# Group B's norm on single columns of tokens, the rotation's transfers on GpSimd's queue, the sums of x on VectorE, and more side steps ahead of transposes, in one step of a hybrid encoder layer

## The chip, the cores and the metric

One core of a Trainium2 chip. The time is device microseconds of a whole execution; of several executions the median is given. The engines of the core are TensorE (PE; its weight loads are PEld), VectorE (DVE), ScalarE (ACT), GpSimd (POOL) and SyncE (SP), which here only issues transfers. Every engine works through its own instructions in order and waits for others by semaphores.

## The reference

One layer for 512 prompt tokens and 8 streams of 16 new tokens, 640 tokens in all, in f32, model width 2048:

```python
xn = rmsnorm(x, norm_mix)
qa, ka, va, qb, kb, vb = split_proj(xn @ w_in)        # widths 1024 x 4, 128, 128
qb, kb = rope_partial(qb, pos), rope_partial(kb, pos) # first 16 of 64 dims of a head
oa = band_attend(qa, ka, va, bias=rel_bias)           # A: 16 heads, own chunk of 64 and 8 before
ob = band_attend(qb, kb, vb, sink=sinks)              # B: 16 q heads on 2 kv heads, window 128
o = concat(rmsnorm(oa, norm_grp_a), rmsnorm(ob, norm_grp_b))
x = x + o @ w_out
h = rmsnorm(x, norm_ffn)
x = x + (silu(h @ w_gate) * (h @ w_up)) @ w_down
return rmsnorm(x, norm_final), ...                    # and the new keys and values
```

The 16 new tokens of a stream attend to a cache of 256 (A) or 128 (B) earlier tokens and to each other; `rmsnorm` is x * rsqrt(mean(x*x) + 1e-6) * g.

## The kernel before

Activations lie transposed: 128 features on the partitions, 640 tokens as two halves of 320 in the columns. Each f32 product of a weight block and an activation tile is three matmuls (`mm3`, L246 to L248): high by high, high by low, low by high, where the high half of the weights is a copy on ScalarE (L237) and the low half a subtraction on VectorE (L238), both 128x1024. `dense` (L258) loads weights, splits them and runs such triples for one block of outputs; its results lie in PSUM tiles named dn, of which there are two, until VectorE multiplies them out. All other PSUM results lie in one of four banks named at.

Most projections into group A, and the feed-forward, go by `quartet`, a scheme of seven products of half size for a product of 2 by 2 blocks, of which the inputs need sums and differences. Those of x are made by `combine` (L943), for eight pairs of tiles: two subtractions on GpSimd (L957, L959), two steps on VectorE (L956, L963), and splits.

The main stream is a sequence of `dense` and `quartet` calls. Side work is written as Python generators, in streams named heads (attention of prompt tokens, `prompt_b` and `prompt_a`), decode (attention of new tokens, `decode_b` and `decode_a`), combine and norm. After each inner step of `dense` a counter rises by `n.rate` (0.55 to 2.5 by stage) and for each whole unit one generator is run to its next `yield`. So a yield more puts more matmuls of the main stream between two pieces of side work, and delays all that the stream does later. A `yield "part"` marks a piece that may be run beside another stream's. Then a scheduler orders each engine's instructions, within rules that keep TensorE's side work at the place where it was written.

In order of time: group B's keys, values and queries are projected, with `rope` (L611) on keys and on the eight query tiles. `rope` fills a tile with zeros on GpSimd, makes four transfers of 8x640 into it through SP's queue (L615, L616), and does three steps on VectorE (L617 to L619). `project_b` stores the new tokens' part of each query tile to memory (`sb_d`, L931), where `decode_b` reads it (L645 on) and GpSimd turns it (L646). `prompt_b` makes scores (L463), their maximum (L466), exponentials on ScalarE (L479), a scaling on VectorE (L484), transposes on TensorE (L376, in `flip`), a copy on ScalarE (L493), and weighs the values (L503). `decode_b` does the same for four steps of two streams each (scores L655, exponentials L668, scaling L673, transposes L376, copies L698, weights by values L707), and stores its output (L718). Then come the quartets, and at the last of them group A's attention starts.

Group B's norm (`norm_b`, L1041) adds the squares of the eight tiles of B's outputs on VectorE (`add`, L883), and runs `wide_steps` (L305), which leaves rsqrt of the mean, 128x640 with equal rows, in `r_b`: one matmul against ones for each half (L311), an affine step (L312), a square root on ScalarE (L314), a reciprocal and a correction in three steps on VectorE (L317 to L320), all on 128x320. The output blocks m = 0, 1, 2, ... of `w_out_b` run meanwhile; the results of m=0 and m=1 wait in the two dn tiles for `r_b` (L1098, then the addition of x, L1099), and m=1's are taken out only after the norm has been written out to its end. Group A's attention and decode run beside it: its copies of turned keys and values are at L629, its exponentials at L479 too, decode A's softmax at L757 to L764 (L761 to L768 after the change, as all lines behind the first edit move by 3, and by 4 to 6 further on).

`rstd_steps` (L276), which group A's norm and the last norm use, gives the same by single columns: matmuls with the tokens as weights and a column of ones as data (L284) give 128 tokens on the partitions and one column for each of six blocks of tokens; the arithmetic on VectorE and ScalarE is on 128x6 (L286 to L291); six matmuls against an identity (L297) spread it back to 128x640, and ScalarE copies it (L303).

## Time and profile before

| | |
|---|---|
| median of 3 runs | 2505.01 us (2503.35 to 2506.9) |
| profiled execution: time, span | 2504.86 us, 2503.1 us |
| granted TensorE clock | 0.998 |
| busy: TensorE, its weight loads | 99%, 96% |
| busy: VectorE, ScalarE, GpSimd | 79%, 42%, 23% |
| mean of memory traffic | 159 GB/s |

The rows of the trace are read so: start in us, length in us, engine, line of the kernel, operation, output and input by their names in the program, shapes, and in brackets the time that the engine stood idle just before and what ended it. The wait tables give, for an instruction and what it waited for, the sum of the idle time, the number of waits and the longest. A matmul with f32 operands leaves two records. Pieces of the chain that ended last have a start, a length and a place.

### The profile page before, as it was taken

The page shows a single profiled execution, that of the slowest core. Times are in us where ns is not written, and L with a number is a line of the kernel's source. Part 1 is how long each engine was busy: PE and PEld are TensorE (multiplying, and loading weights), DVE is VectorE, ACT ScalarE, POOL GpSimd, SP SyncE. Part 2 cuts the span into 40 slices and gives each one's busy share as a digit, 9 for nine tenths or more (in the row PEclk, how much of TensorE's full clock was granted, in tenths as well). Part 3 has the DMA queues.
Part 4 walks back from the last instruction along what each step waited for, and adds up shares of the span by engine and source line. Part 5 has one row for each costly group of instructions (what it writes and reads, how often), then busy time and mean ns, then how long its engine had stood idle before and what let it go on. Part 6 is the DMA issues. An engine that isn't in the chain of part 4 may idle for free.

```text
span 2503.1 us, 44475 instructions
## 1 busy us (share of the span) xinstructions
PE 2470.1 (99%) x17279; PEld 2410.7 (96%) x17279; DVE 1972.3 (79%) x3014; ACT 1056.3 (42%) x1701; POOL 575.7 (23%) x504
## 2 busy tenths in 40 slices
PE   9999999999999999999999999999999999999997
PEld 8888999987899999999999999999999999999997
DVE  7667777785658887788888888888888877777898
ACT  5445333365545543443344343434334333333343
POOL 1001000001002033333333232323232233333212
PEclk9999999999999999999999999999999999999999
DMA  5233533478664334543344344334437765665656
GB/s 200 89 93 119 173 135 125 144 254 288 218 213 158 133 117 147 173 141 121 125 147 133 128 133 143 124 130 132 147 122 237 245 194 167 175 170 167 199 165 195
DMA packets 191123, 401.67 MB, mean 160 GB/s; under 512 B 22496, under 2 KB 83296, under 8 KB 190912
## 3 DMA queue, kind: packets, MB, share of 16 engines
q1 hardware_dynamic: 163888, 339.69, 41.5%
q0 software_dynamic: 23424, 53.59, 7.8%
q10 hardware_dynamic: 3600, 5.55, 0.6%
q8 instruction: 136, 2.23, 0.4%
q14 instruction: 75, 0.61, 0.1%
HBM read 311.14 MB, written 86.87 MB: 159 GB/s over the span
## 4 chain that ended last, share of the span: by engine, by line
PE 91%; DVE 4%; DMA 2%; ACT 1%; issue 1%; POOL 0%; SPq 0%; DVEq 0%; ACTq 0%; POOLq 0%
PE dn L246 18%; PE dn L248 18%; PE dn L247 18%; PE at L246 10%; PE at L248 10%; PE at L247 10%; PE at L376 2%; PE at L503 1%; PE at L463 1%; DVE W L238 1%; DMA W<-w_down 1%; PE at L799 0%; DMA S<-x_d 0%; DVE S L466 0%; ACT W L237 0%
## 5 line engine op out<-in xcount | busy, mean ns | idle before, releaser
L237 ACT ACTIVATE W<-W 128x1024 fp32r<-128x1024 f32 (+2 forms) x662 | 640.5, 968 | 1059.8 <-PE dn L247 570.6
L246 PE MATMUL dn<-S,W 128*128 128x320 f32 x3374 | 1054.2, 313 | 2.0 <-ACT W L237 1.9
L248 PE MATMUL dn<-S,W 128*128 128x320 f32 x3374 | 1043.5, 309 | 1.9 <-DVE W L238 1.9
L247 PE MATMUL dn<-S,W 128*128 128x320 f32 x3374 | 1043.5, 309 | 0.3 <-DVE S L238 0.3
L238 DVE TENSOR_TENSOR W<-W,W 128x1024 fp32r<-128x1024 f32 (+2 forms) x662 | 772.4, 1167 | 95.4 <-ACT W L237 87.7
L246 PEld LDWEIGHTS dn<-S,W 128*128 128x128 f32 x3374 | 633.9, 188 | 17.5 <-issue 13.7
L248 PEld LDWEIGHTS dn<-S,W 128*128 128x128 f32 x3374 | 633.3, 188 | 3.8 <-DVE W L238 2.9
L247 PEld LDWEIGHTS dn<-S,W 128*128 128x128 f32 x3374 | 633.8, 188 | 1.7 <-issue 0.9
L246 PE MATMUL at<-S,W 128*128 128x320 f32 x1834 | 567.1, 309 | 0.7 <-ACT W L237 0.6
L248 PE MATMUL at<-S,W 128*128 128x320 f32 x1834 | 566.9, 309 | 0.6 <-DVE W L238 0.6
L247 PE MATMUL at<-S,W 128*128 128x320 f32 x1834 | 566.7, 309 | 0.0
L246 PEld LDWEIGHTS at<-S,W 128*128 128x128 f32 x1834 | 344.3, 188 | 1.3 <-ACT W L237 1.3
L248 PEld LDWEIGHTS at<-S,W 128*128 128x128 f32 x1834 | 344.3, 188 | 1.2 <-DVE W L238 1.2
L247 PEld LDWEIGHTS at<-S,W 128*128 128x128 f32 x1834 | 344.3, 188 | 0.0
L864 POOL TENSOR_TENSOR W<-W,W 128x1024 f32<-128x1024 f32 (+2 forms) x63 | 138.6, 2200 | 561.0 <-DVE W L238 360.9
L883 DVE TENSOR_TENSOR S<-S,dn 128x320 f32<-128x320 f32 x398 | 182.4, 481 | 73.3 <-PE dn L248 70.8
L883 DVE TENSOR_TENSOR S<-S,at 128x320 f32<-128x320 f32 x292 | 138.4, 483 | 81.8 <-PE at L248 79.2
L873 POOL TENSOR_TENSOR W<-W,W 128x1024 f32<-128x1024 f32 (+2 forms) x63 | 141.9, 2253 | 94.2 <-DVE W L238 93.0
L1176 POOL DMA_DIRECT2D S<-act_d x161 | 86.7, 539 | 282.0 <-PE dn L248 122.6
L857 DVE TENSOR_TENSOR W<-W,W 128x1024 f32<-128x1024 f32 (+2 forms) x86 | 117.2, 1362 | 37.9 <-DMA W<-w_gate 29.0
L861 DVE TENSOR_TENSOR W<-W,W 128x1024 f32<-128x1024 f32 (+2 forms) x86 | 94.6, 1100 | 57.0 <-DMA W<-w_up 30.5
L1240 DVE TENSOR_TENSOR S<-S,half 128x320 fp32r<-128x320 f32 x147 | 119.9, 836 | 2.3 <-ACT half L1238 0.4
(178 smaller groups left out, 1687.4 us busy)
## 6 DMA issues: line engine op xcount, KB each, us to landing
S<-act_d POOLq DMA_DIRECT2D x161, 320.0 KB, 3.7
W<-w_gate SPq DMA_DIRECT2D x88, 512.0 KB
W<-w_up SPq DMA_DIRECT2D x88, 512.0 KB
W<-w_in SPq DMA_DIRECT2D x66, 512.0 KB
W<-w_down SPq DMA_DIRECT2D x64, 384.0 KB
act_d<-half SPq DMA_DIRECT2D x147, 160.0 KB
act_d<-S SPq DMA_DIRECT2D x147, 160.0 KB
W<-w_down SPq DMA_DIRECT2D x68, 320.0 KB
```

The costliest lines, as they stand in the source:

```text
L237: self.nc.scalar.activation(hi, src, AF.Identity)
L238: self.nc.vector.tensor_tensor(lo, src, f(hi), ALU.subtract)
L246: mm(out, a[0], b[0], start=first, stop=False)
L247: mm(out, a[0], b[1], start=False, stop=False)
L248: mm(out, a[1], b[0], start=False, stop=last)
L857: nc.vector.tensor_tensor(b12[:, w], b12[:, w], b22[:, w], sub)
L861: nc.vector.tensor_tensor(s6[:, w], b11[:, w], b12[:, w], sub)
L864: eng.tensor_tensor(b11[:, w], b22[:, w], s6[:, w], sub)
L873: eng.tensor_tensor(b21[:, w], b21[:, w], s6[:, w], sub)
L883: add = lambda o, a, b: nc.vector.tensor_tensor(o, a, b, ALU.add)
L1176: nc.gpsimd.dma_start(out=r(sh(t, 2, HT)), in_=r(act_d[which, :, j]))
L1240: nc.vector.tensor_tensor(r(src), src, hi, ALU.subtract)
```

## The change

Six edits. `prompt_b` gets its mark "part" ahead of the first group of scores, and for the last query tile ahead of both, and one yield more behind the scores of the first and the last tile. `rope` issues its four transfers on GpSimd's queue, and `project_b` its store. `decode_b` gets one more yield ahead of the first turn, and five in place of four ahead of the transposes of each step. `combine` does its two subtractions on VectorE. `norm_b` yields four times in place of once, and uses `rstd_steps`, with six yields behind each of its steps.

```diff
--- before.py
+++ after.py
@@ -557,9 +557,12 @@
         for rr in range(2):
             t0, t1 = n.get("S"), n.get("S")
             heads.append(((t0, t1), [t0[:, 512:640], t0[:, :256], t0[:, 256:512], t1[:, :256]], n.small(4)))
-        yield "part"
         for blocks in ([(0, 0, 128), (1, 0, 256)], [(2, 128, 384), (3, 256, 512)]):
+            if blocks[0][0] == 0 or t == 7:
+                yield "part"
             scores(q, kb, blocks, [mask_b] * 2, heads)
+        if t in (0, 7):
+            yield
         yield
         for rr, (_, es, mx) in enumerate(heads):
             softmax(es, mx, sinks[:, 8 * rr + t:8 * rr + t + 1])
@@ -612,8 +615,8 @@
         rot = n.get("S")
         nc.gpsimd.memset(rot[:80], 0.0)
         for b in (0, 64):
-            dma(out=rot[b:b + 8], in_=x[b + 8:b + 16])
-            dma(out=rot[b + 8:b + 16], in_=x[b:b + 8])
+            nc.gpsimd.dma_start(out=rot[b:b + 8], in_=x[b + 8:b + 16])
+            nc.gpsimd.dma_start(out=rot[b + 8:b + 16], in_=x[b:b + 8])
         nc.vector.tensor_tensor(x[:80], x[:80], cos[:80], ALU.mult)
         nc.vector.tensor_tensor(rot[:80], rot[:80], sin[:80], ALU.mult)
         nc.vector.tensor_tensor(x[:80], x[:80], rot[:80], ALU.add)
@@ -677,13 +680,14 @@
 
         parts = [load(0)]
         yield
+        yield
         turn(parts[0][0], parts[0][3])
         yield "part"
         weights = score(0)
         for step in range(4):
             if step == 0:
                 parts.append(load(1))
-            for _ in range(4):
+            for _ in range(5):
                 yield
             if step == 0:
                 turn(parts[1][0], parts[1][3])
@@ -928,7 +932,7 @@
     def project_b(t):
         q = proj(26 + t, "Q", qps.pop(0) if qps else None, 0.125)
         rope(q)
-        dma(out=sb_d[:, t], in_=q[:, SP:])
+        nc.gpsimd.dma_start(out=sb_d[:, t], in_=q[:, SP:])
         heads_of(prompt_b, t, [("Q", q)], q)
 
     def keep_a(i, p, x):
@@ -942,7 +946,7 @@
 
     def combine(k0, k1):
 
-        tt, st = nc.gpsimd.tensor_tensor, nc.vector.scalar_tensor_tensor
+        tt, st = nc.vector.tensor_tensor, nc.vector.scalar_tensor_tensor
         third = n.get("S" if k0 == 6 else "W")
         for kt in range(k0, k1):
             a, c = n.get("W"), n.get("W")
@@ -1044,9 +1048,11 @@
             add(ssq, ssq, raw_b[t])
             if t % 3 == 0:
                 yield
-        yield
-        for _ in n.wide_steps(ssq, 1024, r_b):
-            yield
+        for _ in range(4):
+            yield
+        for _ in n.rstd_steps({a: [ssq[:, a * HT:a * HT + HT]] for a in range(2)}, 1024, r_b):
+            for _ in range(6):
+                yield
         n.put("S", *raw_b)
 
     for at in range(0, len(order), 2):
```

ScalarE at group B's norm. W_935 and W_936 before, and W_930 and W_931 after, are the raw and the high weights of m=2; S_828 to S_839 are scores of group A's heads; S_845 is `r_b`; rows at L629 and L632 are copies of turned keys and values. Before:

```order
L314 ACT_TABLE_LOAD
L314 ACTIVATE S_871_5654<-S_784_5309 128x640
L237 ACTIVATE W_936_5956<-W_935_5955 128x1024
L629 ACTIVATE W_854_5578<-at_5722 128x512
L629 ACTIVATE W_863_5618<-at_5763 128x512
L629 ACTIVATE S_896_5811<-at_5812 128x512
L479 ACT_TABLE_LOAD
L479 ACTIVATE S_835_5511,sm_5701<-S_835_5511,sm_5700 128x128
```

After, from the fourth head's last two exponentials on; the square root (L287) stands with its table loads between the first head's four exponentials and the second's:

```order
L479 ACTIVATE S_833_5509,sm_5800<-S_833_5509,sm_5799 128x384
L479 ACTIVATE S_832_5508,sm_5800<-S_832_5508,sm_5799 128x512
L303 ACTIVATE S_845_5557<-at_5817 128x320
L303 ACTIVATE S_845_5557<-at_5822 128x320
L632 ACTIVATE S_899_5833<-at_5834 128x512
L632 ACTIVATE S_901_5840<-at_5841 128x512
L237 ACTIVATE W_931_5940<-W_930_5939 128x1024
L493 ACTIVATE S_924_5924<-at_5919 128x512
L763 ACTIVATE S_908_5868,sm_5865<-S_907_5867,sm_5864 128x256
L764 ACTIVATE S_908_5868,sm_5866<-S_907_5867,sm_5864 128x16
```

The split of m=2's weights stood ahead of the sixteen exponentials of four heads, and now stands behind them and behind the two copies into `r_b`.

VectorE at the same place. dn_5564 is the result of m=0, W_937 before and W_932 after are m=2's low weights. Before:

```order
L320 SCALAR_TENSOR_TENSOR S_845_5557<-S_871_5654,S_845_5557 128x320
L772 COPY W_864_5619<-S_865_5622 64x16x16 x2
L1098 TENSOR_TENSOR S_931_5943<-dn_5564,S_845_5557 128x640
L238 TENSOR_TENSOR W_937_5957<-W_935_5955,W_936_5956 128x1024
L1099 TENSOR_TENSOR S_931_5943<-S_931_5943,S_930_5942 128x640
L482 RECIPROCAL sm_5701<-sm_5701 128x4
```

After:

```order
L1104 TENSOR_TENSOR S_926_5927<-dn_5564,S_845_5557 128x640
L762 TENSOR_SCALAR sm_5864<-sm_5864 128x1
L1104 TENSOR_TENSOR S_928_5933<-dn_5730,S_845_5557 128x640
L1105 TENSOR_TENSOR S_926_5927<-S_926_5927,S_925_5926 128x640
L767 TENSOR_TENSOR sm_5865<-sm_5865,sm_5866 128x1
L761 ISA S_917_5894,sm_5891<-at_5886,W_866_5644 128x272
L761 ISA sm_5891 128x1
L768 RECIPROCAL sm_5865<-sm_5865 128x1
L1105 TENSOR_TENSOR S_928_5933<-S_928_5933,S_927_5932 128x640
L762 TENSOR_SCALAR sm_5891<-sm_5891 128x1
L238 TENSOR_TENSOR W_932_5941<-W_930_5939,W_931_5940 128x1024
```

The low half of the weights came directly behind m=0's result; now both results, both additions of x and two steps of decode A's softmax (L767, which reads what L764 leaves, and L768) stand ahead of it.

TensorE at the end of decode B. The rows at L707 (L711 after) are the last weighing of values, dn_2816 and dn_2747 are the projection that runs beside it, whose inner steps take 6 rows each and end with the tile S_71. Before, with the third row behind it:

```order
L707 MATMUL at_2964<-S_507_2901,S_6_86 64x128 x2
L707 MATMUL at_2964<-S_509_2908,S_373_2251 64x128 x2
L707 MATMUL at_2964<-S_509_2908,S_6_86 64x128 x2
L246 MATMUL dn_2816<-S_59_193,W_513_2927 128x320
L247 MATMUL dn_2816<-S_60_194,W_513_2927 128x320
L248 MATMUL dn_2816<-S_59_193,W_514_2928 128x320
```

After:

```order
L711 MATMUL at_2982<-S_515_2955,S_6_86 64x128 x2
L711 MATMUL at_2982<-S_517_2962,S_379_2289 64x128 x2
L711 MATMUL at_2982<-S_517_2962,S_6_86 64x128 x2
L246 MATMUL dn_2747<-S_68_211,W_512_2927 128x320
L247 MATMUL dn_2747<-S_69_212,W_512_2927 128x320
L248 MATMUL dn_2747<-S_68_211,W_513_2928 128x320
```

S_59 is the fifth step from the end of that projection, S_68 the second: 30 rows followed the weighing, and 12 now.

GpSimd's queue at the rotation of the fourth query tile after the change (L616 is the filling with zeros, L618 and L619 the transfers, L935 the store):

```order
L616 MEMSET S_180_1178 80x640
L935 DMA sb_d<-S_134_935 128x128
L616 MEMSET S_218_1408 80x640
L618 DMA S_180_1178<-S_179_1176 8x640
L619 DMA S_180_1178<-S_179_1176 8x640
L618 DMA S_180_1178<-S_179_1176 8x640
L619 DMA S_180_1178<-S_179_1176 8x640
L935 DMA sb_d<-S_179_1176 128x128
L616 MEMSET S_256_1638 80x640
```

Before, GpSimd had the fillings alone there, and the same transfers stood in SP's queue among the loads of weights (L252):

```order
L252 DMA W_199_1299<-w_in 128x1024
L931 DMA sb_d<-S_140_941 128x128
L252 DMA W_223_1434<-w_in 128x1024
L615 DMA S_183_1193<-S_182_1191 8x640
L616 DMA S_183_1193<-S_182_1191 8x640
L615 DMA S_183_1193<-S_182_1191 8x640
L616 DMA S_183_1193<-S_182_1191 8x640
L252 DMA W_234_1514<-w_in 128x1024
L931 DMA sb_d<-S_182_1191 128x128
L252 DMA W_258_1649<-w_in 128x1024
```

The last query's store and the next query's filling now stand ahead of a rotation's transfers, and SP's loads no longer stand behind any of them.

## The prediction

> **What bounds the kernel now.** I read the page first (span, busy time, the chain), then the waits of TensorE, then the timeline around each wait that the diff can reach.

> ```profile
> span 2503.1 us, 44475 instructions
> PE 2470.1 (99%) x17279; PEld 2410.7 (96%) x17279; DVE 1972.3 (79%) x3014; ACT 1056.3 (42%) x1701; POOL 575.7 (23%) x504
> PE 91%; DVE 4%; DMA 2%; ACT 1%; issue 1%; POOL 0%; SPq 0%; DVEq 0%; ACTq 0%; POOLq 0%
> ```

> TensorE works 2470.1 of 2503.1 us, and the chain that ended last lies on it for 91%. Whatever the other engines save counts only where TensorE stands still, and that is 33 us in all. The waits say where:

> ```profile
> PE dn L246 <- ACT S L237: 5.6, 1, 5.6
> PE at L376 <- DVE S L484: 3.2, 3, 1.2
> PE at L311 <- DVE sm L466: 1.5, 1, 1.5
> PE at L376 <- DVE S L673: 1.4, 2, 0.8
> PE at L376 <- ACT S L629: 1.2, 1, 1.2
> PE at L463 <- ACT S L668: 0.9, 1, 0.9
> PE at L655 <- POOL S L646: 0.8, 1, 0.8
> ```

> The columns are the total, the number of waits and the longest. The 5.6 is the start of the program, which the diff leaves alone. The other six rows, 9.0 us, are group B's softmax and transposes, decode B's, and the norm with the first decode transposes of group A. With the 0.5 of a row shown below they make 9.5 us: all that the change can win, 0.38% of the time. One of them, L629 in decode A (588.39), lies behind the norm.

> ```profile
> 89.28 0.70 PE L376 MATMUL at<-cst,S 128*128 128x128 f32 x3 [1.07 <-DVE S L484]
> 208.32 0.76 PE L655 MATMUL at<-S,S 64*128 64x144 f32 x8 [0.77 <-POOL S L646]
> 277.93 0.42 PE L248 MATMUL dn<-S,W 128*128 128x320 f32 x1 [0.51 <-DVE W L238]
> 530.62 1.34 PE L311 MATMUL at<-S,gains 128*128 128x320 f32 x4 [1.53 <-DVE sm L466]
> 547.07 0.30 PE L376 MATMUL at<-cst,S 128*128 128x128 f32 x1 [1.16 <-DVE S L484]
> 548.29 0.30 PE L248 MATMUL dn<-S,W 128*128 128x320 f32 x1
> ```

> Each row is start, length, and in brackets the idle time ahead of it. Up to 255 us these waits make 5.0 us (9.0 less 1.53, 1.16 and 1.2 at the norm and behind it, to rounding); 2.7 stand at the norm.

> **The norm (edit 6): TensorE's own work.**

> ```profile
> 53.00 1.08 PE at L311 x4
> 726.33 1.23 PE at L284 x12
> 728.39 0.15 PE dn L248
> ...
> 731.03 0.15 PE dn L248
> 731.33 1.28 PE at L297 x12
> 535.31 2.15 DVE L317 RECIPROCAL S<-S 128x320 f32<-128x320 f32 x1
> ```

> All but the last are pieces of the chain: two matmuls against ones (four records) took 1.08; group A's norm, which already goes by single columns, took 1.23 for six column sums and 1.28 for six spreads. Between the two dense matmuls shown lie 18 in 2.64, 0.147 each. The change swaps the first for the other two: 1.23 + 1.28 - 1.08 = +1.4 us on the bounding engine, with nothing to hide it. VectorE loses some 7 us of wide work (the reciprocals alone are two of 2.15, in the last row) and gets seven small ones; that is a gain only if TensorE waits for it.

> **The norm: what moves.** ScalarE does its work in order, and here the order decides:

> ```profile
> 538.18 1.06 ACT L237 ACTIVATE W<-W 128x1024 fp32r<-128x1024 f32 x1 [4.46 <-DMA W<-w_out_b]
> 540.74 0.60 ACT L629 ACTIVATE S<-at 128x512 f32<-128x512 f32 x1 [0.53 <-PE at L376]
> 541.36 1.28 ACT L479 ACT_TABLE_LOAD   x1
> 542.65 0.40 ACT L479 ACTIVATE S<-S,sm 128x128 f32<-128x128 f32 x1
> 544.85 0.39 ACT L479 ACTIVATE S<-S,sm 128x128 f32<-128x128 f32 x1
> 731.98 0.44 ACT L303 ACTIVATE S<-at 128x320 f32<-128x320 f32 x1 [3.18 <-PE at L297]
> 543.82 0.82 DVE L1098 TENSOR_TENSOR S<-dn,S 128x640 f32<-128x640 f32 x1
> 544.56 1.22 DVE L238 TENSOR_TENSOR W<-W,W 128x1024 fp32r<-128x1024 f32 x1
> ```

> Before, the high half of the weights of m=2 (L237) is made at 538.18, ahead of all exponentials, and its low half (L238) at 544.56. TensorE uses both in the row at 548.29, with time to spare. After, L237 stands behind all sixteen exponentials and r_b's two copies, as the order fences in the section on the change show. Worked out in the times of before: the last group of scores waits for its banks as L311 did (1.5 of the 2.7 us stays), the last score is read at about 534.1, and ScalarE then has, without a gap, four exponentials (544.85 - 542.65 = 2.2), a table load 1.28, a short Sqrt 0.25, a copy of flips 0.6, a table load 1.28, eight exponentials 4.4, a copy 0.6, four exponentials 2.2, two copies to r_b 0.9, two of flips 1.2, and L237 1.06: 16.0 us, to 550.1. VectorE's L238 is behind L767, which waits for L764, and that stands behind L237, a copy and an exponential on ScalarE (1.3). After it come L767, L761, L768, L1105 (as wide as L1098, 0.8), L762, some 1.8 together, and L238 itself 1.2. So the low half is ready at 550.1 + 1.3 + 1.8 + 1.2 = 554.4. TensorE would reach that row at about 549.2 + 0.6 for the three or four rows ahead of it: it stops there for some 4.5 us. Against 548.29 the row is 6.1 us late, of which 0.7 is work done ahead (flips, two rows of m=3). **+5.4 us**, the 1.4 of work and the two waits of before taken into account. The ends: if L237 were late by r_b's copies alone (1.4 work, 1.0 of wait, less 1.2) it is +1; if the loads that L237 and L1105 read come later by half of the 4.46 that ScalarE waited for one at 538.18, +7.5. I take 5.4, since every piece of the chain has a row. These four heads' exponentials now end some 4 us earlier (547.0 for 551), so the 1.2 at 588.39 may go: between -1.2 and 0, I take -0.4.

> **Ahead of the norm (edits 1, 3, 4).** Extra yields put dense matmuls between what makes an operand and what reads it. Decode B's transposes come 4 to 7 rows later (15 for 11, 24 for 17, 42 for 36), 0.6 to 1.0 us, against waits of 0.9, 0.55 and 0.84: these go, -2.2. At 89.28 the scores stand 9 rows earlier, the table load no longer behind a weight split: -1.0. At 188.24 (0.92) the flips move by 3 rows, 0.4. At 208.32 the turn of the queries has 8 rows more, 1.2 us, but the store of q7 goes through another queue: between -0.8 and +1, I take 0. Together -3.5, at least -2, at most -5.0.

> What is late next is the end of decode B. Its last matmul stands 12 rows ahead of the end of its projection, where it had 30: 18 x 0.147 = 2.6 us nearer to what depends on it:

> ```profile
> 255.44 6.62 DMA ob_d<-W
> 262.07 4.68 DMA W<-xT
> ```

> In this chain the store frees the buffer into which xT is loaded, then come a sum and VectorE's splits up to L238 at 277.93, where TensorE waited 0.51 already. A chain that starts 2.6 us later against the same rows gives the wait back at 3.1. So of -3.5 about **-0.9** is left; with the bounds, between +0.6 and -5.0 (if the chain has room that the wait of 0.51 hides).

> **The sums of x (edit 5).**

> ```profile
> L957 POOL TENSOR_TENSOR W<-W x8: 878/882/1066, 41.5 to 267.4; 128x320 f32<-128x320 f32 x8
> L963 DVE SCALAR_TENSOR_TENSOR W<-W,gains x8: 541/552/1164, 42.4 to 268.5; 128x320 f32<-128x320 f32 x8
> 267.24 0.48 DVE L238 TENSOR_TENSOR S<-W,S 128x320 fp32r<-128x320 f32 x1
> ```

> GpSimd needs 0.88 for a subtraction and VectorE waits for it; by the 0.48 that VectorE's splits of 320 columns take, two of them per step cost 0.96 in place of a wait of 1.06. In the chain above that is 0 within 0.3. Nothing on TensorE waits for VectorE in the first 60 us, so 0 there. L963 took 1.16 once while GpSimd worked, 0.55 otherwise; that goes, and is worth nothing off the path. [...]

> **Rotation on GpSimd's queue (edit 2).**

> ```profile
> L615 SPq DMA_DIRECT2D S<-S x18: 624/642/798, 63.9 to 194.3; - x18
> L1176 POOL DMA_DIRECT2D S<-act_d x161: 527/528/709, 1914.6 to 2463.2; - x161
> S<-act_d POOLq DMA_DIRECT2D x161, 320.0 KB, 3.7
> 73.63 0.62 SPq L616 DMA_DIRECT2D S<-S  x1
> 76.11 0.81 DVE L617 TENSOR_TENSOR S<-S,S 80x640 f32<-80x640 f32 x1
> ```

> Nine rotations of four transfers leave SP (0.64 each, 23 us in all) for GpSimd, whose issue took 0.53. SP's loads behind them get away earlier; no TensorE wait up to 255 us names a weight load, so nothing is won. On SP the last issue began at 73.63 and L617 ran at 76.11: at most 2.5 us. On GpSimd such a transfer, of larger data, landed 3.7 us after issue. It can be up to 1.2 later for each rotation, or earlier by 4 x 0.11. Behind L617 on VectorE stand L466, L474 and the weights' L238, so a late rotation is paid where TensorE waits already: at 89.28 and 188.24. Between 0 and +2.4; I take +0.2, since SP's queue of 12 transfers in a row at the start gets shorter.

> [...]

> **Sum:** 5.4 - 0.4 - 0.9 + 0.2 = +4.3 on the profiled execution (2503.1 in the span, 2504.9 with what lies around it). Its time is 0.15 under the median of the runs, 2505.01, so I forecast 2505.0 + 4.3 = **2509.3**, 0.17% more. What a measurement of this kernel can tell from no change is about 0.2%, 5.0 us: 2500.0 and 2510.0 are the bounds.

> **Rivals.**
> *The early waits stay won.* If the chain behind decode B has room, the whole 5.0 is kept: 5.4 - 0.4 - 5.0 = 0, 2505. For it: its first piece is a store that landed after 6.6 us, most of it waiting in queues that the change empties. Against it: the wait of 0.51 shows that the chain is at its limit.
> *The norm is no stop.* If ScalarE got to L237 before TensorE needs m=2 (its exponentials wait for nothing and L303 is quick), both waits of 2.7 go, 1.4 of work comes: -1.3 there, with the early part at -3 to -5 and the 1.2: -5.5 to -7.5, 2498.5, faster. It needs 4.5 us of ScalarE's 16 to vanish, and every piece is measured.
> *Slower: the rotations are late.* GpSimd's transfers land 1.2 later for each of the rotations on the path, and the scores behind L617 hold the transposes: the two waits of softmax grow by 2.4 in place of vanishing (-1.5). It decides from 0.7 us of delay at each, and gives 4.3 + 2.2 + 1.5 = +8: 2513. [...]

> **How the numbers follow.** Likeliest, the sum, 0.50, its own range 2506 to 2512, three fifths of it under 2510.0. The early waits won: 0.17, all within 0.2%. No stop at the norm: 0.12, nine tenths of it faster. Late rotations: 0.21, all slower. Faster 0.11; same 0.30 + 0.17 + 0.01 = 0.48; slower 0.20 + 0.21 = 0.41. The range takes in the second and most of the fourth case: 2502 to 2513.5 leaves out the third and the end of the fourth.

> **What would show it.** A new wait of TensorE for L238's lower half (dn, L248) of 4 to 5 us near 550; L237 at about 549 on ScalarE behind L303; waits L376 <- L673 and L463 <- L668 gone; a wait of about 3 us for L238 near 278 in place of 0.51; L311 gone from 530. The forecast is wrong if the wait near 550 is under 2 us, if the one near 278 has not grown, or if L617 is waited for by TensorE's scores.

## The result, and the profile after

The changed kernel took 2518.76 us (median of 6, 2518.19 to 2521.8) against 2504.91 of the kernel before: 13.9 us more, a ratio of 1.0055 with a 95% interval of 1.0045 to 1.0066. The forecast was 2509.3, in a range of 2502 to 2513.5. The page of the profiled execution (2518.19 us) and its waits of TensorE:

```profile
span 2516.3 us, 44529 instructions
PE 2476.2 (98%) x17299; PEld 2419.0 (96%) x17299; DVE 1968.0 (78%) x3025; ACT 1056.3 (42%) x1703; POOL 584.3 (23%) x532
```

```profile
PE at L658 <- POOL S L649: 5.1, 1, 5.1
PE dn L246 <- ACT W L237: 3.4, 4, 1.5
PE dn L248 <- DVE W L238: 2.8, 4, 1.1
PE at L463 <- DVE sm L466: 2.4, 4, 1.1
PE at L376 <- DVE S L484: 1.3, 4, 0.5
PE at L376 <- DVE S L675: 0.2, 1, 0.2
```

The waits for the softmax's scaling (L484) and for decode B's (3.2 and 1.4 before; L675 was L673) have mostly gone. In their place stands one of 5.1 us at decode B's first scores, and L237, L238 and L466 have become longer. The timeline at the two places, and the chain that leads to the first:

```profile
212.20 1.09 PE L658 MATMUL at<-S,S 64*128 64x144 f32 x6 [5.10 <-POOL S L649]
551.49 0.38 PE L246 MATMUL dn<-S,W 128*128 128x320 f32 x1 [0.52 <-DVE sm L762]
553.54 0.63 PE L246 MATMUL dn<-S,W 128*128 128x320 f32 x1 [1.53 <-ACT W L237]
555.35 0.63 PE L248 MATMUL dn<-S,W 128*128 128x320 f32 x1 [0.90 <-DVE W L238]
```

```profile
200.75 6.87 DMA sb_d<-S
...
207.74 3.67 DMA S<-sb_d
...
211.53 0.62 POOL S L649
```

The last query tile's store to `sb_d` was issued at 200.75 and landed 6.87 us later; only then could SP load it, and GpSimd turn it. At the norm ScalarE and VectorE did what the order had said:

```profile
548.64 0.74 ACT L303 ACTIVATE S<-at 128x320 f32<-128x320 f32 x2
549.27 1.06 ACT L632 ACTIVATE S<-at 128x512 f32<-128x512 f32 x2
550.23 1.05 ACT L237 ACTIVATE W<-W 128x1024 fp32r<-128x1024 f32 x1
554.08 1.21 DVE L238 TENSOR_TENSOR W<-W,W 128x1024 fp32r<-128x1024 f32 x1
```

What the forecast did not have is in the column PEclk of the table by stretches (behind the busy times of PE, PEld, DVE, ACT and POOL come the granted clock, the share of the transfer engines and GB/s):

```profile
207.00:210.00 3.00, 0.10 (x1) 0.00 (x0) 2.46 (x4) 0.31 (x1) 0.00 (x0) 1.00 0.17 40
212.00:214.00 2.00, 1.80 (x14) 1.80 (x16) 0.41 (x2) 0.00 (x0) 0.76 (x2) 0.54 0.55 205
214.00:216.00 2.00, 2.00 (x10) 1.35 (x9) 1.37 (x9) 1.31 (x6) 0.00 (x0) 0.60 0.00 0
...
558.00:560.00 2.00, 2.00 (x10) 1.96 (x9) 0.00 (x0) 0.86 (x2) 0.00 (x0) 0.50 0.91 294
562.00:564.00 2.00, 2.00 (x19) 1.99 (x17) 0.00 (x0) 1.36 (x3) 0.42 (x2) 1.00 0.31 77
```

Behind each of the two stops TensorE ran at half its clock (0.50): the matmuls of 128x320 began 0.27 us apart there (558.55, 558.82, 559.08) and 0.147 apart at full clock. The stretches are 3.4 us long (from 212.17) and 6.8 us (from 553.51). TensorE worked for 3.4 and 5.9 us of them; half of that, 1.7 and 2.9 us, is what they cost at most. Before the change there is no such stretch up to the last matmul.

So the 13.2 us between the two spans come from: 6.1 more of TensorE's busy time, of which 1.4 is the norm's matmuls and the other 4.7 nearly all the half clock; 5.4 of TensorE's idle time (the turn of the queries +4.3, the norm 4.6 for 2.7, stretches between 590 and 690 3.0 for 1.2, the other waits up to 279 -2.3, the start -0.4); and 1.7 behind the last matmul (12.8 for 11.1).

### The profile page after: what moved, and what is told of

The parts are those of the page before. It is cut to its first block, busy times and chain, and to the rows that moved or that the text cites. A ratio compares the mean times of both kernels' runs of the same rounds, so it can differ in the third digit from the quotient of the medians.

```text
span 2516.3 us, 44529 instructions
## 1 busy us (share of the span) xinstructions
PE 2476.2 (98%) x17299; PEld 2419.0 (96%) x17299; DVE 1968.0 (78%) x3025; ACT 1056.3 (42%) x1703; POOL 584.3 (23%) x532
## 4 chain that ended last, share of the span: by engine, by line
PE 90%; DVE 4%; DMA 2%; issue 2%; ACT 2%; POOL 1%; POOLq 0%; ACTq 0%; DVEq 0%; SPq 0%
PE dn L246 18%; PE dn L248 18%; PE dn L247 18%; PE at L247 10%; PE at L246 10%; PE at L248 10%; PE at L376 2%; PE at L503 1%; ACT S L479 1%; PE at L463 1%; DVE S L466 1%; DVE W L238 1%; DMA W<-xT 0%; PE at L803 0%; DVE S L238 0%
## 5 line engine op out<-in xcount | busy, mean ns | idle before, releaser
L237 ACT ACTIVATE W<-W 128x1024 fp32r<-128x1024 f32 (+2 forms) x662 | 640.6, 968 | 1058.3 <-PE dn L247 581.6
L246 PE MATMUL dn<-S,W 128*128 128x320 f32 x3374 | 1054.3, 313 | 4.2 <-ACT W L237 3.4
L248 PE MATMUL dn<-S,W 128*128 128x320 f32 x3374 | 1045.1, 310 | 2.8 <-DVE W L238 2.8
L238 DVE TENSOR_TENSOR W<-W,W 128x1024 fp32r<-128x1024 f32 (+2 forms) x662 | 770.8, 1165 | 92.5 <-ACT W L237 87.8
L246 PEld LDWEIGHTS dn<-S,W 128*128 128x128 f32 x3374 | 634.5, 188 | 18.6 <-issue 12.1
L248 PEld LDWEIGHTS dn<-S,W 128*128 128x128 f32 x3374 | 634.0, 188 | 6.2 <-DVE W L238 4.2
L246 PE MATMUL at<-S,W 128*128 128x320 f32 x1834 | 567.1, 309 | 0.8 <-ACT W L237 0.6
L248 PE MATMUL at<-S,W 128*128 128x320 f32 x1834 | 566.9, 309 | 0.5 <-DVE W L238 0.5
L246 PEld LDWEIGHTS at<-S,W 128*128 128x128 f32 x1834 | 344.3, 188 | 1.3 <-ACT W L237 1.3
L248 PEld LDWEIGHTS at<-S,W 128*128 128x128 f32 x1834 | 344.3, 188 | 1.0 <-DVE W L238 1.0
```

Of the source, the lines that this page charges most:

```text
L237: self.nc.scalar.activation(hi, src, AF.Identity)
L238: self.nc.vector.tensor_tensor(lo, src, f(hi), ALU.subtract)
L246: mm(out, a[0], b[0], start=first, stop=False)
L248: mm(out, a[1], b[0], start=False, stop=last)
```

## The experiments

Times are given as differences to the kernel before in the same comparison, whose median lay between 2505.2 and 2506.2.

### The norm: columns or yields

The norm's edit was undone in the changed kernel, and made alone in the kernel before:

```diff
 a_norm_old (changed kernel)
-        for _ in range(4):
-            yield
-        for _ in n.rstd_steps({...}, 1024, r_b):
-            for _ in range(6):
-                yield
+        yield
+        for _ in n.wide_steps(ssq, 1024, r_b):
+            yield
 b_norm (kernel before): the same lines the other way round
```

> The changed kernel with group B's norm as before (one yield, wide_steps). Theory: the norm costs 1.4 us of matmuls, 1.9 us of waits more than before near 550, 3 us of half clock behind them and 2.4 us of waits between 590 and 690 that the shift of group A's heads brings: together 8.7, so the time falls from 2518.8 to about 2510. Rival (the clock and the waits behind 590 come from elsewhere): it falls by 1.4 + 1.9 = 3.3, to 2515.5.

> The kernel before with the one edit of group B's norm (four yields, single columns, six yields behind each step). Theory: the same 8.7 us as in the changed kernel, 2505 to about 2513.5, with waits for L238 and L237 near 550 and a clock near 0.5 for 5 to 6 us behind them. Rival (work alone): 2506.4. If only the wait moves and the clock stays full: 2508 to 2510.

Measured: a_norm_old +2.5 us (1.0011, 1.0002 to 1.002), 11.4 under the changed kernel (10.1 between the two medians themselves), where 8.7 was expected; b_norm +7.7 (1.003, 1.0019 to 1.0042), for 8.7 expected. The norm's edit is the largest part. Alone it shows the wait and the clock side by side:

```profile
552.13 0.64 PE L246 MATMUL dn<-S,W 128*128 128x320 f32 x1 [3.91 <-ACT W L237]
```

```profile
551.50:552.00 0.50, 0.00 (x0) 0.00 (x0) 0.50 (x4) 0.50 (x2) 0.00 (x0) 0.59 0.78 287
552.00:558.00 6.00, 5.34 (x20) 4.50 (x20) 3.70 (x10) 3.00 (x8) 1.41 (x2) 0.50 0.87 285
558.00:558.50 0.50, 0.50 (x4) 0.50 (x3) 0.00 (x0) 0.22 (x1) 0.00 (x0) 0.58 0.94 352
```

The half clock lasts from about 551.6 to 558.4, 6.8 us, of which TensorE works 5.8: it costs 2.9 at most. This execution has 3.4 us more of it from 1957.9, behind waits of 0.44 and 1.13 us that the kernel before has there too (0.44 and 1.14), at full clock.

Then columns and yields were set apart, in the kernel before:

```diff
 b_norm11: single columns, few yields
+        yield
+        for _ in n.rstd_steps({...}, 1024, r_b):
+            yield
 b_wide46: 128x320 as before, many yields
+        for _ in range(4):
+            yield
+        for _ in n.wide_steps(ssq, 1024, r_b):
+            for _ in range(6):
+                yield
```

> The kernel before with the norm on single columns, but with one yield ahead of it and one behind each of its steps in place of four and six. On ScalarE the split of m=2's weights (L237) then stands ahead of group A's exponentials and only behind the two copies into r_b. Theory (the yields put the weights behind the exponentials; the columns cost only their 1.4 us of matmuls): no wait over 1.2 us between 528 and 600, clock full there, time within 2 us of before, 2506. Rival (the single columns themselves, through r_b's chain over TensorE, VectorE and ScalarE): waits of 4 us and the half clock as with the whole edit, 2513.

> The kernel before with only the yields of the norm: four ahead of it and six behind each step, but the norm on 128x320 as before. L237 of m=2 stands behind all sixteen exponentials, and the results of m=0 and m=1 wait for the norm. Theory (yields): waits of 3 us or more near 550, a half clock behind them, 2509 to 2516. Rival (single columns): no such wait, 2505 to 2507.

Measured: b_norm11 +2.7 (1.0009, 1.0001 to 1.0018), b_wide46 +16.8 (1.0066, 1.0053 to 1.0078). With few yields the columns cost 2.7 us, 1.4 of which is their matmuls (the expectation was at most 2), and the clock stays at 1.0:

```profile
528.00:560.00 32.00, 30.14 (x246) 27.55 (x246) 22.57 (x81) 20.67 (x59) 2.69 (x10) 1.00 0.66 225
```

With many yields and the wide norm it is far worse, also than the 2509 to 2516 us that were expected. The waits of b_wide46, from its timeline:

```profile
549.85 1.12 PE L376 MATMUL at<-cst,S 128*128 128x128 f32 x4 [2.55 <-ACT S L629]
556.44 0.61 PE L246 MATMUL dn<-S,W 128*128 128x320 f32 x1 [5.47 <-DVE sm L758]
```

There the second wait ends on VectorE, which reached the last step of `r_b` (L320) only at 553.38 and multiplied m=0's result out of its dn tile from 555.49 to 556.30: both dn tiles were full until then. So the yields are the cause, and in their company the single columns are the better norm. The four yields ahead of the norm and the six behind each step were not set apart.

The forecast's step was that TensorE waits for m=2's weights. They were split earlier, with the norm's whole edit in place:

```diff
 b_norm_pre2
+        if m == 1:
+            early = [n.weights(io["w_out_b"][k], 8) for k in (1, 2)]
-        psb.append((m, n.dense([(io["w_out_b"][m], 8)], acts_b)))
+        psb.append((m, n.dense([early.pop(0) if early else (io["w_out_b"][m], 8)], acts_b)))
```

> The kernel before with the whole edit of the norm, and the weights of m=2 loaded and split together with those of m=1. On ScalarE L237 of m=2 then stands behind one head's exponentials in place of four, and r_b's copies where they were. Theory (the weights are what TensorE waits for): the wait near 548 falls from 3.9 to under 2 us, the clock stays full, and the time falls from 8.3 over before to 3 to 5 over. Rival (the two dn tiles, which r_b frees, are what it waits for): the wait stays at 3 us or more and the time at 7 to 8 over.

Measured: +2.4 (1.0014, 1.0005 to 1.0022), 5.3 less than b_norm. L237 ran at 542.56 in place of 551.01; r_b's copies came at 548.36 (b_norm: 546.46), no earlier. The wait of 3.91 became these two, and the clock stayed full there:

```profile
548.87 1.31 PE L748 MATMUL at<-S,W 128*32 128x272 f32 x16 [0.79 <-issue]
551.12 0.41 PE L246 MATMUL dn<-S,W 128*128 128x320 f32 x1 [0.94 <-DVE sm L758]
```

The weights were what it waited for; the dn tiles are next, 0.9 us.

### The half clock

To see whether the clock follows from the wait, the wait was filled with work:

```diff
 b_norm_fill (kernel before with the norm's edit)
+        if m == 2:
+            idle = n.bank()[:, :HT]
+            for k in range(20):
+                nc.tensor.matmul(idle, acts_b[0][0][:, :P], acts_b[0][0][:, :HT], ...)
```

> The kernel before with the whole edit of the norm, and 20 dense matmuls of 320 columns with an unused result ahead of the block m=2, where TensorE waited for 3.9 us. They add work that the output does not need. Theory (a wait that empties about half of a stretch of 3.4 us halves the clock for the next one or two, apart from the wait itself): the waits there shrink to some 1 us, the clock stays at 1.0 between 548 and 562, and the time falls by 3 us from that of the norm's edit alone (8.3 us over before) to about 5 over. Rival (the lower clock is not from the wait): the time stays at 8 over, or rises.

```profile
549.00:553.00 4.00, 3.71 (x30) 2.94 (x21) 4.00 (x12) 4.00 (x13) 0.21 (x1) 1.00 0.03 10
553.00:557.00 4.00, 2.37 (x14) 1.84 (x15) 3.98 (x11) 2.19 (x6) 1.30 (x2) 1.00 0.87 267
557.00:563.00 6.00, 6.00 (x50) 5.98 (x49) 0.00 (x0) 3.94 (x8) 0.11 (x1) 1.00 0.93 310
```

The clock stays at 1.0, where it was 0.50 in b_norm from about 551.6 to 558.4: there it fell because of the empty time. From the end of the matmuls at L748 to a later row that both have (the seven transposes at 560.41 and at 559.83) this took 12.2 us of b_norm and 10.3 here. The time was +7.6, though, as with b_norm and not the 5 expected: in the profiled execution it had lost 1.3 us against b_norm by 531, ahead of the place, and the other runs don't show where. The local gain is shown, that of the whole time is not.

### The late store

The store went back to SP's queue; decode B's yields were undone; the single yield ahead of the first turn alone was taken out (with the norm as before); and the transfers were moved alone, in the kernel before, all of them or only the stores:

```diff
 a_sbd_sp (changed kernel)
-        nc.gpsimd.dma_start(out=sb_d[:, t], in_=q[:, SP:])
+        dma(out=sb_d[:, t], in_=q[:, SP:])
 a_dec_old (changed kernel): one yield less ahead of the first turn, and
-            for _ in range(5):
+            for _ in range(4):
 a_no_d1 (a_norm_old)
         parts = [load(0)]
         yield
-        yield
 b_rope_sbd (kernel before): rope's four transfers and the store by nc.gpsimd.dma_start
 b_sbd (kernel before): the store by nc.gpsimd.dma_start
```

> The changed kernel with one edit undone: the store of each query tile's new tokens to sb_d goes by SP's queue again, the rotations stay on GpSimd's. In the changed kernel TensorE waits 5.1 us at L658, because the last such store, issued at 200.75, landed only at 207.6, and the clock is halved for 3 us behind that wait. Theory A (the queue): on SP the store lands in under 4.5 us, the wait falls under 2 us, the half clock there goes, and the time falls by 4 to 6 us from 2518.8 to about 2514. Rival B (the loads of the two caches, which now stand directly ahead of the store and fill the 16 transfer engines): the store lands late on SP too, the wait stays over 4 us and the time within 1 us of 2518.8.

> The changed kernel with decode_b's yields as before (one ahead of the turn, four ahead of transposes). Rival B of the late store (the cache loads moved next to it by the extra yields): the store of the last query lands in under 4.5 us and the wait at L658 falls under 2 us; with the waits for L673 and L668 back (2.2 us) the time falls by 2 to 4 us, to about 2516. Theory A (the queue): the wait at L658 stays at 4 to 6 us, the other waits come back, and the time rises by 1 to 2 us, to about 2520.

> The changed kernel with the norm as before and without the one yield that was added ahead of decode B's first turn; the transfers stay on GpSimd's queue and the five yields ahead of transposes stay. In SP's order the loads of the two caches then stand away from the last store to sb_d. Theory (the added yield brings the cache loads beside the store, which lands late in their company): the store lands in under 4.5 us, the wait at L658 falls from 4.4 to 2.5 or less, and the time is 2 to 4 us under that of the changed kernel with the old norm (2508.6, 3.0 over before in its comparison). Rival (GpSimd's queue is late by itself): the wait stays at 4 or more and the time within 1 us of that.

> The kernel before with only the transfers moved: the rotations' and the stores to sb_d on GpSimd's queue. Here the loads of the two caches stand 8 us ahead of the last store, not beside it. Theory A (GpSimd's queue is late by itself): the rotations land 3.5 us behind their last issue where SP's took 2.3, the last store lands after 5 us or more, the wait ahead of the scores of decode B (0.8 before) grows to 3 or more, the time rises by 3 to 6 us, to 2510. Rival B (the late store is from the loads beside it): the store lands in 2 to 4 us, the wait stays under 2 us, the time within 1.5 us of 2506.

> The kernel before with only the eight stores to sb_d on GpSimd's queue. If the longer end of the program comes from any transfer more on that queue: the stretch behind the last matmul is 12.8 us as with all transfers. If it comes from the rotations' 36: 11.1 as before. The store lands in 4 us or less, with no cache load beside it, and the time is within 1 us of before.

SP issues the load of `sb_d` (L640 before, L643 after) when the last store has landed, and GpSimd turns what it brings. The table has both steps; the last three runs, described in the part on the yields below, have all transfers on SP's queue, and of them only early_sp has the yield ahead of the first turn:

| | last store issued to loaded again, us | load issued to turned | wait at the scores | half clock near 210 costs, at most | time |
|---|---|---|---|---|---|
| before | 3.8 (SP) | 3.7 | 0.8 | 0 | 0 |
| changed kernel | 7.0 (GpSimd) | 3.8 | 5.1 | 1.7 | +13.9 |
| a_sbd_sp | 5.7 (SP) | 3.7 | 3.0 | 0 | +9.4 |
| a_norm_old | 6.4 (GpSimd) | 3.6 | 4.4 | 2.4 | +2.5 |
| a_dec_old | 2.0 (GpSimd) | 5.3 | 1.8 | 1.7 | +10.7 |
| a_no_d1 | 2.0 (GpSimd) | 5.0 | 1.7 | 1.7 | +0.1 |
| b_rope_sbd | 4.0 (GpSimd) | 3.6 | 2.7 | 1.7 | +3.5 |
| b_sbd | 3.5 (GpSimd) | 3.6 | 0.9 | 0 | +0.8 |
| early_sp | 2.5 (SP) | 7.6 | 2.5 | 0 | +0.7 |
| p_d2 | 2.2 (SP) | 6.9 | 2.5 | 0 | +3.6 |
| p_d2_c | 3.0 (SP) | 6.5 | 1.7 | 0 | +0.4 |

With the added yield ahead of the first turn and the rotations on GpSimd's queue the store takes 5.7 to 7.0 us on either queue; without that yield 2.0 to 4.0 on GpSimd's. So GpSimd's queue is the smaller part of the delay: SP's gave back 1.3 of 7.0, and the wait of 3.0 in a_sbd_sp lies between what theory A and rival B had expected. In SP's order the yield puts the loads of the two caches and of a weight block (1 MB, issued from 197.4 to 199.8 in the changed kernel) directly ahead of the store; before, the caches' stood 10 us ahead. The caches' loads, which rival B names, are not enough: in early_sp they were issued 1.6 and 0.9 us ahead of the store, which landed in 2.5 us, and the load behind it was late instead, from its chain:

```profile
198.69 2.45 DMA sb_d<-S
...
201.20 7.50 DMA S<-sb_d
```

What goes with a late transfer in all eleven traces is the weight block. Whichever of the two, the store or the load behind it, was issued 0.4 to 1.2 us behind a load of weights took 5.0 to 7.6 us, and every other one 2.0 to 4.0. No run moved that load alone, so this is read off and not tested. With the yield out (a_no_d1) the time is 2.4 under a_norm_old. The last rotation is late by itself, as the chain of b_rope_sbd shows (its time, +3.5, fits theory A, its store of 4.0 us rival B):

```profile
193.06 3.79 DMA S<-S
...
207.74 0.60 POOL S L646
```

The last transfer of the last rotation landed 3.8 us behind its issue, close to the 3.7 of the forecast's row; on SP's queue, in the kernel before, L617 ran 2.3 us behind that issue (194.95 and 197.22). The queries were turned at the same time as before (207.74 for 207.66), while TensorE came 1.9 us sooner (205.7 for 207.6), and waited for what it had won; the half clock then cost it 1.7.

The rotations also lengthen the end of the program. The stretch behind the last matmul is 12.8 us in all five kernels with all the transfers moved, 12.2 where only the rotations are, and 10.5 to 11.2 in all others, b_sbd with 11.1 among them. GpSimd's last drain is what is longer, first before, then after:

```profile
L1559 POOLq DRAIN  x3: 40/93/9161, 2492.5 to 2502.8; - x3
L1565 POOLq DRAIN  x3: 46/97/11527, 2504.0 to 2516.1; - x3
```

Why 36 small transfers at 70 to 195 us make a drain at 2504 longer stays open.

### The yields and the sums of x ahead of the quartets

```diff
 p_d2 (kernel before): prompt_b's yields of the change, and
-            for _ in range(4):
+            for _ in range(5):
 p_d2_c: p_d2, and in combine
-        tt, st = nc.gpsimd.tensor_tensor, nc.vector.scalar_tensor_tensor
+        tt, st = nc.vector.tensor_tensor, nc.vector.scalar_tensor_tensor
 early_sp: p_d2_c, and the yield ahead of decode B's first turn
 b_sums (kernel before): the line of combine alone
```

> The kernel before with prompt_b's yields and the five yields ahead of decode B's transposes, and nothing else. The waits for L484, L673 and L668 go as in the changed kernel, and the turn of the queries waits as before (0.8 to 1.8). If nothing is given back at the first quartet: 3 us under before. By the prediction's part on the end of decode B, 0.9 under.

> The same as the last with the sums of x on VectorE. By the prediction's part on the sums: the same time within 1 us. Rival (VectorE is later at the last sums, which the first quartet waits for): 1 to 2 us more.

> The yields of prompt_b and decode_b and the sums of x on VectorE, with all transfers on SP and the norm as before. If the waits up to 255 us go as in the prediction's part on them and nothing is given back at the first quartet (the wait for L238 near 278 stayed at 0.5 in the changed kernel): 2506 - 3 = 2503. If the turn of the queries waits for the store beside the loads of the caches even on SP: a wait of 2 to 4 us at L658 and 2506 to 2508.

> The kernel before with only the sums of x on VectorE. By the prediction: no change within 0.5 us. If the sums are a part of the chain that the first quartet waits for: the wait for L238 near 277 (0.5) goes, and 0.5 to 1 us of time. The 3 us that they took off beside decode B's yields are then theirs only because the yields had put that chain on the path.

Measured: p_d2 +3.6 (1.0018, 1.0009 to 1.0027), p_d2_c +0.4 (1.0006, 0.9997 to 1.0015), early_sp +0.7 (1.0002, 0.9993 to 1.0011), b_sums **-3.4** (0.9988, 0.9979 to 0.9997). The yields slow the kernel, and the sums on VectorE are what makes it faster: b_sums, at 2502.2, beats both kernels. The times of p_d2, p_d2_c and b_sums lie outside what was expected for them; early_sp's is as the second of its two cases had it. In p_d2 little is won at all: up to 282 us the waits for L484 are 2.8 us (2.0 before), those for decode B's scaling 1.6 (1.4), the turn of the queries 2.5 (0.8), and only the wait for L668 (0.9) is gone. Then the first quartet waits 2.7 us where it waited 0.5:

```profile
209.83 0.76 PE L658 MATMUL at<-S,S 64*128 64x144 f32 x8 [2.49 <-POOL S L649]
280.81 0.39 PE L246 MATMUL dn<-S,W 128*128 128x320 f32 x1 [2.19 <-DVE S L448]
281.86 0.41 PE L248 MATMUL dn<-S,W 128*128 128x320 f32 x1 [0.51 <-DVE W L238]
```

In b_sums no wait of TensorE over 0.15 us is left between 212 and 506. The waits of VectorE there, before (240 to 276 us) and with the sums moved (238 to 273):

```profile
DVE W L963 <- POOL W L957: 2.9, 3, 1.1
DVE W L857 <- DMA W<-w_in: 2.0, 1, 2.0
```

```profile
DVE S L959 <- ACT W L955: 1.1, 1, 1.1
```

VectorE stood for GpSimd's subtraction three times, 2.9 us, and everything behind L963 in its order stood too, the splits for the first quartet among it. The last L963 began at 268.50 before and at 263.60 in b_sums, and the wait of 0.51 at 278 is gone.

These three waits ended at 251.74, 257.49 and 268.50, too late for TensorE's waits for decode B's scaling (L673), which ended at 226.54 and 249.11. There VectorE did not stand; its own steps ran long beside a subtraction on GpSimd. Before, and the same two steps in b_sums:

```profile
224.87 0.99 POOL L959 TENSOR_TENSOR W<-W 128x320 f32<-128x320 f32 x1 [0.68 <-ACT W L955]
225.02 0.85 DVE L670 TENSOR_TENSOR sm<-sm,sm 128x1 f32<-128x1 f32 x1
246.68 1.16 DVE L963 SCALAR_TENSOR_TENSOR W<-W,gains 128x320 f32<-128x320 f32 x1
```

```profile
223.89 0.15 DVE L670 TENSOR_TENSOR sm<-sm,sm 128x1 f32<-128x1 f32 x1
245.12 0.55 DVE L963 SCALAR_TENSOR_TENSOR W<-W,gains 128x320 f32<-128x320 f32 x1
```

An addition of one column took 0.85 us in place of 0.15 and ended with GpSimd's subtraction (225.87 and 225.86), and L673 stands behind it. Ahead of 249 an L672 (0.60 for 0.28) and the L963 shown lost 0.9 us together, against a wait of 0.84. Both waits are gone in b_sums. With the one at 278 that is 1.9 of the 3.4 us; the rest lies in differences of 0.4 us and less.

## Why the prediction was wrong, point by point

- **The norm's chain: mechanism and place right, its price too small.** L237 behind the exponentials and r_b's copies, L238 behind L767, the stop of m=2: forecast in the times of before for 549 to 550.1 and 554.4 at its end, found at 550.23 and 555.35, with TensorE 2.4 us late on arrival at that part. In b_norm, where TensorE came in time, the stop was 4.4 us (3.91 and 0.49) for the 4.5 of the forecast, though mostly for L237 and not for L238. In the changed kernel the idle time rose by 1.9 and the work by 1.4; but the step that failed was to price a stop by its length. The half clock behind it cost up to 2.9 more, and the shifted heads 1.9 between 590 and 690, where the forecast had a gain of 0.4. The term of +5.4 measured 7.7 alone and 11.4 in the changed kernel (13.9 less a_norm_old's 2.5). The rival by which the weights come in time did not happen.
- **The store through GpSimd's queue: taken at 0, with +1 as its end.** The wait at L658 rose by 4.3, and 1.7 of half clock followed. The forecast looked at the queue and not at what the added yield moved beside the store: SP's loads of the caches and of a weight block. What was late next was asked for the end of decode B and not for its start.
- **The rotations: +0.2 for +3.5 (with the stores).** Their landing was known from the row (3.7, measured 3.8 for the last one); it was spent not at L484, as the slower rival had it, but at the turn of the queries, and by half clock and at the end of the program, which nothing in the forecast held.
- **The sums of x: 0 for -3.4.** The step compared 0.96 of work with 1.06 of wait for one step of the sums. Only one of its two subtractions lies on the chain, and behind a wait (three here, 2.9 us) everything in VectorE's order waits. The long L963 beside GpSimd's work (1.16) was seen and put at nothing "off the path"; but such long steps stand ahead of L673, and they were the cause of the waits for L673 that the forecast gave to the yields.
- **Decode B's yields: -3.5, and -0.9 after the quartet, for about +4** (p_d2 +3.6; early_sp against b_sums 4.1). The giving back near 278 was right as long as the sums were on GpSimd: 2.7 us in p_d2 for a forecast of 3.1. In the changed kernel the moved sums paid for it, and the wait stayed at 0.5. What failed ahead of that is that the yields alone did not remove the waits for L484 and L673 (4.4 us in p_d2, 3.4 before). Of early_sp's 4.1 us its trace, 2.4 us under its median, shows 0.7 as idle time, and the mean granted clock of its runs (0.9967, b_sums 0.9975) makes some 1.8; where the rest lies stays open.
- **The forecast's own signs.** L237 behind L303, L673 and L668 gone, L311 gone from 530: these came. Two did not: the wait for L238 at L248 near 550 was 0.90 and not 4 to 5 us, with 1.53 for L237 ahead of it, and the wait near 278 did not grow. So the sum was wrong in its parts and not only in its total.
- The sign and the order of size at the norm were right; a forecast that slowed by 4.3 met 13.9, since the norm, the store and the rotations carried a second cost that was left out.

The price that the forecast lacked is that of the half clock: 3.4 and 6.8 us of it in the changed kernel, and 3.4 us in a_dec_old behind a gap of TensorE of 1.79 us; see the last section.

## What to carry to other kernels

Price a stop of TensorE by its length and by the half clock that can follow it: here 3.4 us of it behind a stop of 1.79 us (a_dec_old) and one of 5.10 (the changed kernel), at a cost of up to 1.7 us, 6.8 us behind those near 550 (the changed kernel and b_norm), at up to 2.9, and none behind one of 3.01 (a_sbd_sp). Where a yield more is put ahead of something, read each queue for what the delayed work now stands beside or behind; a weight split for the next block belongs ahead of side work that nobody is waiting for. Where an engine waits for a slower one (0.88 us on GpSimd for a subtraction of 128x320 that takes 0.49 on VectorE), count its whole queue as waiting, look whether its own steps run long beside the slower one's (0.85 us for 0.15 here), and move the operation to the engine that waits if it has the time.

## What the runs showed of the hardware

```profile
203.67:207.09 3.42, 1.63 (x16) 1.23 (x16) 1.26 (x2) 0.73 (x1) 1.06 (x2) 1.00 0.39 89
207.09:210.50 3.41, 3.41 (x18) 1.96 (x18) 2.17 (x12) 2.00 (x8) 0.17 (x1) 0.50 0.40 133
```

```profile
206.98:210.39 3.41, 1.96 (x14) 1.70 (x12) 1.69 (x4) 1.06 (x1) 0.00 (x0) 1.00 0.55 136
210.39:213.81 3.42, 1.86 (x19) 1.53 (x20) 1.78 (x4) 0.41 (x3) 1.47 (x2) 1.00 0.56 138
```

The wait of 1.79 lies in one stretch of 3.42 us, of which TensorE was busy for 1.63; the one of 3.01 is spread over two, with 1.96 and 1.86. In a_norm_old the clock fell at 209.45, in the middle of the wait from 207.1 to 211.4.

These stretches are read off the traces. In each of the seventeen, all later changes of the clock lie whole multiples of 3.413 us behind the first; in the changed kernel it fell at 212.17 and at 553.51, 100 of them apart. So every trace can be cut into such windows. Of some 12000 windows at full clock between 12 and 2480 us, the clock fell behind all eleven in which TensorE's records fill less than 0.495, behind four of the nine between 0.495 and 0.545, and behind none of the others. It came back behind a full window, and not behind those that further waits left at most 0.81 full, which makes 6.8 us out of 3.4; one full window of b_wide46 (from 641.9, mostly scores on 64 partitions) did not bring it back either. No run varied a wait by itself, so no threshold is measured.

So such a stop cost more in one execution than in another: behind the waits of 0.44 and 1.13 us near 1957 the clock was halved for 3.4 us in b_norm, behind those of 0.44 and 1.14 us in the kernel before it was not. The runs of a_norm_old reach from 2506.2 to 2513.8, those of the kernel before from 2504.4 to 2507.9 in the same comparison. In p_d2 the execution shown took 2508.2 us at a mean clock of 0.998, the longest one 2514.2 at 0.994.

Steps of VectorE ran long beside GpSimd's without any wait in the tables: an addition of 128x1 on VectorE took 0.85 us beside a GpSimd subtraction of 128x320 and 0.15 without it. By what mechanism is not shown.
